# Experts' weights in 2 MB pieces with 16 KB runs: nine whole buffers, and rows and columns taken in fours

## The chip, the core and the metric

The kernel runs on one core of a Trainium2 chip. The metric is the device time of one execution in microseconds (us). TensorE (PE) does the matmuls; before each of them it loads a stationary operand, which the profile lists apart as PEld. VectorE is DVE, ScalarE is ACT, GpSimd is POOL. SyncE (SP) issues nearly all transfers from the chip's memory (HBM) into the on-chip memory of 128 partitions (SBUF). MB here is 1,048,576 bytes, and KB 1,024.

## What is computed

One layer of an encoder on 272 rows, 16 meta tokens and 256 inputs; only the 256 are returned, so only they go through the experts here: two mixers side by side (attention and a state-space scan), an output projection, a layer norm, then a mixture of 32 experts of which each row takes four, and a last layer norm. The change touches the experts alone:

```python
def expert_block(args):                       # one block of rows of one expert e
    tok, g, e = args
    xb = t_pad[tok]
    gate = xb @ w_gate[e] + b_gate[e]         # 1024 x 1024, fp32, as are the next two
    up   = xb @ w_up[e] + b_up[e]
    gate = jnp.minimum(gate, 7.0)
    up   = jnp.clip(up, -7.0, 7.0)
    y = ((up + 1.0) * gate * jax.nn.sigmoid(gate * 1.702)) @ w_down[e] + b_down[e]
    return (y * g[:, None]).astype(t.dtype)
```

The weights of 32 experts are 32 x 3 x 4 MB = 384 MB, and every one of them is read once in a run.

## The kernel before

**Two halves.** Until about 190 us the mixers, the projections and the router run. Then the experts follow, in 32 *positions*. A position is one expert, chosen at run time by how many rows it got, with one or more *units* of 128, 64 or 32 row slots (6, 13 and 14 units in all). For each position the work on PE is: gather the rows, gate, up, and down of the position before.

**The stream of weights.** SP loads the weights in the order gate and up of position t, then down of position t - 1. A piece is 1 MB: 256 rows of a 1024 x 1024 matrix, two whole rows in each of the 128 partitions, so one run of 8 KB per partition. The `ring` of lines 515 to 516 names 19 half buffers of 1 MB; the tiles in them are called wx. They stand on the places of tiles of the first half of the kernel, so the ring comes free one by one. `chunk` (lines 530 to 557) issues one piece, `load_to` (line 559) issues up to a count. A piece may be issued when the piece 19 places before it has been read for the last time, that is, when PE has finished two of the eight blocks of 128 rows (`kb`) of that matrix. The very last piece is issued as two of 512 KB. Four slots (0, 2, 5, 8: `HALVED`) are two tiles of 1 MB each, the others one tile of 2 MB; half of slot 9 is the 19th piece, its other half holds tables.

**The three matmuls.** `linear` (line 1188): the rows are stationary, the weights move. One fp32 matmul stands in the trace as two records, each with a load of its own. With 128 slots, the outputs are two runs of 512 columns. With 64 slots two groups of PE columns work on 512 weight columns each, and with 32 slots four groups on 256 columns each (*quarters*), so the result of a 32-slot unit is folded into 128 partitions x 256 columns.

**Whose row is where.** Since a partition holds neighbouring rows 2p and 2p + 1 of a piece, block kb of the contraction holds rows 256 j + 2p + k. Whatever multiplies the weights must be laid out alike. `rows_of` (line 511) gives these rows as a slice with a step of two columns, 8 bytes apart, and it is used in two places as stationary operand: `token_cols` (line 1151), which gathers the rows of a group of units and turns them (matmuls of `hr` with a one-hot matrix, line 1157: 8 blocks x 2 halves x 2 records = 32 loads in a group, 16 groups), and `transposed` (line 1229), which turns the result of gate and up before down (line 1236: one load per block of 128, 2 for a unit of 32, 4 for one of 64, 8 for one of 128).

**Order.** Each engine's order is that of the code. SP's queue is one: a piece that waits for its buffer holds all pieces behind it. Behind position 28 a loop (`overflow`, line 1305) does what exceeds the slots; SP enters it too, so a limit on `load_to` keeps the pieces issued ahead of it to those that PE still needs there and a few more. `linear` on PE waits for each piece's transfer.

Of the kernel before, what the change touches and what calls it, by code (L numbers as in the profile page):

```python
# [21 lines left out]
D = 1024  # L22
# [42 lines left out]
def hybrid_layer(ctx, tc, I, out):  # L65
# [18 lines left out]
    def slot(i, shape, name, dt=F32):  # L84
        return per.tile(shape, dt, name=name, tag=f"slot{i}")

    HALVED = (0, 2, 5, 8)

    def parts4(i, name, dt=F32):

# [26 lines left out]


    hr = per.tile([128, 2, D], F32, name="hr", tag="hr")
    xs5 = [slot(f"5{c}", [128, 2048], "xs5") for c in "ab"]  # L120
    xm = xs5[1][:16, 1024:2048]
    VR = pt([48, 128], "VR")
    VP = et([48, 128], "VP")
# [48 lines left out]
    s8a, s8b = slot("8a", [128, 2048], "s8a"), slot("8b", [128, 2048], "s8b")  # L172
    oh = s8b[:32, 1600:1600 + NB]
    load(oh, "bucket_onehot", 0, [[NB, 32], [1, NB]])
    load_win("k", 2, 512, 2)
# [294 lines left out]
    BAT = [slot(f"5{c}", [128, 16, 128], "BAT") for c in "ab"]  # L470
    for ri in range(2):
        for a in range(4):
            b = nb()
# [7 lines left out]
                S.activation(BAT[ri][:, 4 * a:4 * a + 4], srcv, AF.Copy)  # L481


    sl0 = slot("0a", [128, 2, D], "sl0")
# [24 lines left out]


    def rows_of(kb):
        a = 256 * (kb // 2) + kb % 2
        return slice(a, a + 255, 2)

    ring = [(9, 0), (6, 0), (6, 1), (3, 0), (3, 1), (4, 0), (4, 1), (2, 0), (8, 0), (2, 1), (8, 1), (1, 0), (1, 1),
            (5, 0), (0, 0), (5, 1), (0, 1), (7, 0), (7, 1)]
    NR = len(ring)
    RT, CH, eid, npools = {}, {}, {}, {}
    stream = []
    for t in range(NE):  # L520
        stream += [(t, w, j) for w in range(2) for j in range(4)]
        if t:
            stream += [(t - 1, 2, j) for j in range(4)]
    stream += [(NE - 1, 2, j) for j in range(4)]
    place = {x_: c for c, x_ in enumerate(stream)}

    def chunk(c):
        t, w, j = stream[c]
        i, half = ring[c % NR]
        if i not in RT:  # L530
            if i == 7:
                t_ = npools["b"].tile([128, 4, D], F32, name="wx", tag="slot7")
                RT[i] = [t_[:, 0:2], t_[:, 2:4]]
            elif i == 9:
                RT[i] = [slot("9a", [128, 2, D], "wx")]
            elif i in HALVED:
                RT[i] = [slot(f"{i}{c}", [128, 2, D], "wx") for c in "ab"]
            else:
                t_ = slot(i, [128, 4, D], "wx")
                RT[i] = [t_[:, 0:2], t_[:, 2:4]]  # L540
        CH[c] = RT[i][half]
        src = I[("w_gate", "w_up", "w_down")[w]]
        if t < 2:
            srcv = pap(src, t * D * D + j * 256 * D, [[2 * D, 128], [1, 2 * D]])
        else:
            if t not in eid:
                eid[t] = SP.value_load(EI[0:1, t:t + 1], min_val=0, max_val=NE - 1)
            srcv = src[0][ds(eid[t], 1), j * 256:(j + 1) * 256, :].rearrange("o (p k) f -> p (o k f)", p=128)
        dstv = CH[c].rearrange("p k f -> p (k f)")
        if c < len(stream) - 1:  # L550
            SP.dma_start(dstv, srcv)
        else:
            for k in range(2):
                SP.dma_start(dstv[:, k * D:(k + 1) * D], srcv[:, k * D:(k + 1) * D])

    nload = [0]

# [2 lines left out]
            chunk(nload[0])  # L560
            nload[0] += 1

    load_to(1)


    def split_w(j, s_, l_, ks):
# [107 lines left out]
    value_rows(0, vt0)  # L674
    states_a(3)
    W_HI, W_LO, W_OUT = {}, {}, {}
    wo1 = [slot(f"2{c}", [128, 2, D], "wo1") for c in "ab"]
    W_OUT[1] = [t_[:, k] for t_ in wo1 for k in range(2)]
    for j in range(2):
        load(wo1[j], "w_out", (512 + 256 * j) * D, [[D, 128], [128 * D, 2], [1, D]])  # L680
    scores_b(2, 0)
    scores_b(2, 1)
    states_b(3)
# [527 lines left out]
    gk = {64: 1, 32: 0}  # L1211

# [16 lines left out]
    def transposed(u_, m):  # L1229
        nf = 128 // m  # L1230
        for a in range(u_.shape[1]):
            nk = u_.shape[2] // 128
            b = 6 + misc[0]
            misc[0] ^= 1
            for k in range(nk):
                T.transpose(PS[:, b, k * 128:k * 128 + 128], u_[:, a, rows_of(k)], ident)  # L1236
            V.tensor_copy(yT[:, 4 * a:4 * a + nk], PS[:, b, :nk * 128].rearrange("p (k s) -> p k s", k=nk))  # L1237
        if m == 128:
            return lambda kb: yT[:, kb]
        q = 8 // nf  # L1240
        return lambda kb: yT[:, kb % q, (kb // q) * m:(kb // q) * m + m]
# [63 lines left out]
    def overflow():  # L1305
        n = nc.values_load(nover[0:1, 0:1], min_val=0, max_val=64)
        with tc.For_i(0, n) as i:  # L1307
            m = 64
            e = SP.value_load(tabi[0:1, 1, ds(i, 1)], min_val=0, max_val=NE - 1)
            t = V.value_load(tabi[0:1, 0, ds(i, 1)], min_val=0, max_val=NE - 1)  # L1310
            pc, gc = wt([128, 2], "pc"), wt([128, 2], "gc")
            th = wt([128, 1], "th")
            V.tensor_copy(th, tabs[:, 1, ds(i, 1)])
            V.tensor_copy(pc, PMs[:, :, ds(t, 1)].rearrange("p a b -> p (a b)"))
            V.tensor_copy(gc, Gs[:, :, ds(t, 1)].rearrange("p a b -> p (a b)"))
            V.tensor_scalar(pc, pc, th, None, op0=OP.subtract)
            sel = wt([96, 128], "si", BF, bufs=3)
            V.tensor_copy(sel[:, :m], P96[:, ds(t, 1)].to_broadcast([96, m]))
            oh_, go = wt([128, 2, 128], "ohp", bufs=2), wt([128, 2, 128], "gop")
            for a in range(2):  # L1320
                V.tensor_scalar(oh_[:, a, :m], io[:, :m], pc[:, a:a + 1], None, op0=OP.is_equal)
                V.tensor_scalar(go[:, a, :m], io[:, :m], pc[:, a:a + 1], gc[:, a:a + 1], op0=OP.is_equal, op1=OP.mult)
            xg = wt([128, 8, 128], "xgp", tag="xg1")
            token_cols(xg, oh_, m)
            gt = gate_rows(go, m)

            def streamed(w):
                tiles = {}
# [32 lines left out]
    def out_pos(t):  # L1361
        for u in pos_units[t]:
            unit_out(u)
        for g in range(NG):
            if last_pos[g] == t:
                combine(g)
        if t == LOOP_AT:
            sum_pending()
            overflow()
        load_to(place[t, 2, 3] + 1 + NR)  # L1370

    def first_done():
        sort_b()
# [178 lines left out]
```

## Time and profile before

| | before |
|---|---|
| median of 3 runs | 1146.16 us (1142.4 to 1146.54) |
| profiled execution: own time | 1143.38 us |
| profiled execution: span of the trace | 1141.6 us |
| mean granted PE clock | 0.95 |
| PE busy | 1022.5 us, 90 % |
| PE weight loads (PEld) | 527.3 us, 46 % |
| weight pieces (gate, up, down) | 128 + 128 + 127 of 1 MB, 2 of 512 KB |
| one piece from issue to landing | 19.7 to 19.8 us |
| moved from HBM | 423.5 MB (of 10^6 bytes), 373 GB/s over the span |

The span runs from the first to the last instruction; the execution's own time is 1.8 us longer. Views of the trace used below: *busy by stretch* (for a stretch of the span, its length, then for each engine the busy us and in brackets the instructions, the granted clock of PE, where 1.00 is 2.4 GHz and 0.50 is 1.2 GHz, the busy share of the DMA engines, GB/s); *waits* (who waited, for whom, us in total, times, the longest); *groups of instructions by shape* (line, engine, operation, output<-input, partitions x elements, count, then busy us, mean ns of one, then idle time before them and what ended it). A load's mean ns is its latency; loads and matmuls overlap, so what one costs a busy PE is read from how often the next begins.

### The profile page before, as it was taken

To read this page: it belongs to the slowest core of one execution; us is meant where nothing else is said; L and a number is where in the kernel's file an instruction comes from. 1 tells how busy PE (TensorE), PEld (TensorE's weight loads), DVE (VectorE), ACT (ScalarE), POOL (GpSimd) and SP (SyncE) were. 2 spreads that over 40 slices of the span, in tenths; PEclk is the share of its full clock that TensorE was granted. 3 is DMA by queue.
4 is the path that set the end of the run, shared out by engine and by line. 5 is a ranking of instruction groups with operands and counts; after the bars stand their busy time and mean duration, and the time that the engine had idled before them with its cause. 6 is when DMAs were issued, how large, how long until landed. Compare 5 with 4: busy or idle time off the path is not lost. (4 is left out here: it accounts for less than half of the span.)

```text
span 1141.6 us, 16410 instructions
## 1 busy us (share of the span) xinstructions
PE 1022.5 (90%) x6572; PEld 527.3 (46%) x6572; DVE 365.6 (32%) x755; ACT 159.6 (14%) x329; POOL 106.5 (9%) x223
## 2 busy tenths in 40 slices
PE   6986997899999788997999977799999999998665
PEld 5865884344554344445444433344453444453222
DVE  7999664222122212321131221122222212222103
ACT  1734423000010000111001000010000000001000
POOL 2300004101100110021001010101101010010001
PEclk9999897999999989998999988999999999999779
DMA  7824286999999999999999999999999999999894
GB/s 220 288 96 167 94 341 253 385 375 420 421 421 421 421 420 420 422 420 421 421 421 420 420 421 420 421 421 421 421 421 421 421 421 394 423 419 420 329 419 195
DMA packets 72313, 425.67 MB, mean 373 GB/s; under 512 B 14925, under 2 KB 15546, under 8 KB 23210
## 3 DMA queue, kind: packets, MB, share of 16 engines
q1 hardware_dynamic: 72234, 424.58, 91.3%
q8 instruction: 53, 0.87, 0.3%
q14 instruction: 26, 0.21, 0.1%
HBM read 423.50 MB, written 1.87 MB: 373 GB/s over the span
## 5 line engine op out<-in xcount | busy, mean ns | idle before, releaser
L1204 PE MATMUL PS<-wx,xgp 128*32 128x256 f32 (+2 forms) x3008 | 484.3, 492 | 38.8 <-DMA wx<-in_w_gate 19.5
L1204 PEld LDWEIGHTS PS<-wx,xgp 128*32 128x32 f32 (+2 forms) x3008 | 185.0, 133 | 296.4 <-issue 203.0
L1204 PE MATMUL PS<-wx,yT 128*32 128x256 f32 (+2 forms) x1504 | 231.0, 473 | 8.8 <-DMA wx<-in_w_down 8.0
L1204 PEld LDWEIGHTS PS<-wx,yT 128*32 128x32 f32 (+2 forms) x1504 | 91.5, 129 | 133.6 <-issue 93.4
L946 POOL COPY si<-P 96x32 bf16<-96x32 bf16 (+2 forms) x32 | 7.4, 233 | 754.8 <-PE PS L1198 724.9
L1251 DVE COPY yc<-PS 32x256 f32<-32x256 f32 (+1 forms) x39 | 20.0, 514 | 159.6 <-ACT yc L1253 159.6
L1157 PEld LDWEIGHTS PS<-ohp,hr 128*128 128x128 f32 x512 | 65.8, 206 | 9.6 <-issue 9.6
L1157 PE MATMUL PS<-ohp,hr 128*128 128x128 f32 x512 | 68.1, 294 | 0.2 <-DVE ohp L1149 0.2
L1226 DVE TENSOR_SCALAR PS<-PS 128x256 f32<-128x256 f32 (+2 forms) x33 | 22.6, 684 | 123.4 <-PE PS L1204 123.4
L1198 PE MATMUL PS<-B,si 96*32 96x256 bf16 (+2 forms) x282 | 40.4, 340 | 16.7 <-SPq L1307 9.7
L1220 DVE TENSOR_SCALAR g<-PS 128x256 f32<-128x256 f32 (+1 forms) x27 | 14.9, 553 | 114.4 <-PE PS L1204 100.6
L1253 ACT ACTIVATE yc<-PS 32x256 f32<-32x256 f32 (+1 forms) x39 | 17.4, 446 | 239.0 <-PE PS L1204 232.7
L1237 DVE COPY yT<-PS 128x512 f32<-128x512 f32 (+1 forms) x39 | 22.7, 594 | 85.6 <-PE PS L1236 85.6
L1288 DVE SCALAR_TENSOR_TENSOR lo<-yc,gc,hi 128x1024 fp32r<-128x1024 f32 x15 | 19.3, 1285 | 86.7 <-ACT hi L1287 85.5
L1302 DVE TENSOR_TENSOR acc<-PS,acc 128x1024 f32<-128x1024 f32 x30 | 35.4, 1220 | 16.6 <-PE PS L1299 16.4
L1161 ACT ACTIVATE xgp<-PS 128x512 f32<-128x512 f32 x16 | 9.6, 598 | 216.4 <-PE PS L1157 216.4
L1198 PEld LDWEIGHTS <-si 96*32 96x32 bf16 (+2 forms) x282 | 11.5, 102 | 50.3 <-issue 47.8
L1147 POOL TENSOR_SCALAR gop<-io,PMs,Gs 128x32 f32<-128x32 f32 (+2 forms) x60 | 33.1, 565 | 0.0
L1221 ACT ACTIVATE PS<-g 128x256 f32<-128x256 f32 (+1 forms) x27 | 13.2, 491 | 138.4 <-DVE g L1220 138.4
L1220 DVE TENSOR_SCALAR yc<-PS 128x1024 f32<-128x1024 f32 x6 | 7.3, 1225 | 78.4 <-PE PS L1204 78.4
L1299 PE MATMUL PS<-hi,gt 128*128 128x512 f32 x60 | 26.6, 443 | 3.0 <-ACTq L1307 3.0
L1299 PE MATMUL PS<-lo,gt 128*128 128x512 f32 x60 | 25.1, 419 | 0.7 <-DVE lo L1288 0.7
(389 smaller groups left out, 845.9 us busy)
## 6 DMA issues: line engine op xcount, KB each, us to landing
wx<-in_w_gate SPq DMA_DIRECT2D x128, 1024.0 KB, 19.8
wx<-in_w_up SPq DMA_DIRECT2D x128, 1024.0 KB, 19.8
wx<-in_w_down SPq DMA_DIRECT2D x127, 1024.0 KB, 19.7
w_u<-in_w_in SPq DMA_DIRECT2D x2, 1024.0 KB
w_q<-in_w_in SPq DMA_DIRECT2D x1, 2048.0 KB
w_k<-in_w_in SPq DMA_DIRECT2D x2, 1024.0 KB
w_v<-in_w_in SPq DMA_DIRECT2D x1, 2048.0 KB
wo<-in_w_out SPq DMA_DIRECT2D x2, 1024.0 KB
```

The source lines that it names most:

```text
L1147: eng.tensor_scalar(dst[:, i, o:o + m], iv, pc, gg[:, i, t:t + 1], op0=OP.is_equal, op1=OP.mult)
L1157: T.matmul(PS[:, 4 + h, k * 128:k * 128 + n], hr[:, i, rows_of(db)], oh_[:, i, :n], start=(i == 0), stop=(i == 1))
L1198: T.matmul(o, sel[:, :m], B96[:, w, f * n:f * n + n], start=True, stop=False)
L1204: T.matmul(PS[(f % nf) * m:(f % nf) * m + m, b + f // nf, :n], xT(kb), c[:, f * n:f * n + n], start=False, stop=(kb == 7))
L1220: V.tensor_scalar(g_, r_, 7.0, None, op0=OP.min)
L1226: V.tensor_scalar(r_, r_, 7.0, -7.0, op0=OP.min, op1=OP.max)
L1237: V.tensor_copy(yT[:, 4 * a:4 * a + nk], PS[:, b, :nk * 128].rearrange("p (k s) -> p k s", k=nk))
L1251: V.tensor_copy(d_, s_)
L1253: S.activation(d_, s_, AF.Copy)
L1288: V.scalar_tensor_tensor(lo[:n], YC[g][:n], GC[g][:n], hi[:n].bitcast(F32), op0=OP.mult, op1=OP.subtract)
L1299: T.matmul(PS[:, 4 + 2 * i + h], GT[g][:n, i * 128:(i + 1) * 128], part[:n, h * 512:(h + 1) * 512], start=(j == 0), stop=(j == 1))
L1302: V.tensor_tensor(acc[:, i].rearrange("p (h c) -> p h c", h=2), PS[:, 4 + 2 * i:6 + 2 * i], acc[:, i].rearrange("p (h c) -> p h c", h=2), ...
```

## The change

Pieces become 2 MB: 512 rows, four neighbouring rows per partition, one run of 16 KB in HBM and in SBUF. The ring is nine whole buffers of 2 MB (18 MB in all); half of slot 9 is no longer used, and no slot is halved (`HALVED = ()`). A matrix is then two pieces, and a buffer comes free when PE has finished four blocks. The first piece is issued behind two transfers of `w_out` instead of ahead of them. The last piece is issued as 1 MB, 512 KB, 512 KB.

Block kb now holds rows 512 j + 4p + k. So `rows_of` steps by four columns, 16 bytes; the load in `token_cols` does, and that in `transposed` for units of 64 and 128 slots. For units of 32 slots the load in `transposed` keeps a step of two, because the quarters of gate and up are taken otherwise: quarter f holds two of every four columns of its half (`cols`, `place_of`), so the moving operand reads pairs of columns, 8 bytes of every 16. Down keeps whole quarters. The loop behind position 28 reads its rows to match.

```diff
-    HALVED = (0, 2, 5, 8)
+    HALVED = ()
...
     def rows_of(kb):
-        a = 256 * (kb // 2) + kb % 2
-        return slice(a, a + 255, 2)
-
-    ring = [(9, 0), (6, 0), (6, 1), (3, 0), (3, 1), (4, 0), (4, 1), (2, 0), (8, 0), (2, 1), (8, 1), (1, 0), (1, 1),
-            (5, 0), (0, 0), (5, 1), (0, 1), (7, 0), (7, 1)]
+        a = 512 * (kb // 4) + kb % 4
+        return slice(a, a + 509, 4)
+
+    ring = [6, 3, 4, 2, 8, 1, 5, 0, 7]
...
     for t in range(NE):
-        stream += [(t, w, j) for w in range(2) for j in range(4)]
-        if t:
-            stream += [(t - 1, 2, j) for j in range(4)]
-    stream += [(NE - 1, 2, j) for j in range(4)]
+        stream += [(t, w, j) for w in range(2) for j in range(2)]
+        if 0 < t < NE:
+            stream += [(t - 1, 2, j) for j in range(2)]
+    stream += [(NE - 1, 2, j) for j in range(2)]
...
-            srcv = src[0][ds(eid[t], 1), j * 256:(j + 1) * 256, :].rearrange("o (p k) f -> p (o k f)", p=128)
+            srcv = src[0][ds(eid[t], 1), j * 512:(j + 1) * 512, :].rearrange("o (p k) f -> p (o k f)", p=128)
...
-        if c < len(stream) - 1:
-            SP.dma_start(dstv, srcv)
-        else:
-            for k in range(2):
-                SP.dma_start(dstv[:, k * D:(k + 1) * D], srcv[:, k * D:(k + 1) * D])
+        for k0, k1 in (((0, 4),) if c < len(stream) - 1 else ((0, 2), (2, 3), (3, 4))):
+            SP.dma_start(dstv[:, k0 * D:k1 * D], srcv[:, k0 * D:k1 * D])
...
-    load_to(1)
...
-    load_to(19)
+    load_to(9)
...
+        def cols(a, f):
+
+            if m > 32 or w == 2:
+                return a[:, f * n:f * n + n]
+            return a[:, f // 2 * 512:f // 2 * 512 + 512].rearrange("p (q e k) -> p e q k", e=2, k=2)[:, f % 2]
+
+        def place_of(f):
+            o = PS[(f % nf) * m:(f % nf) * m + m, b + f // nf, :n]
+            return o if m > 32 or w == 2 else o.rearrange("p (q k) -> p q k", k=2)
...
             for f in range(1024 // n):
-                T.matmul(PS[(f % nf) * m:(f % nf) * m + m, b + f // nf, :n], xT(kb),
-                         c[:, f * n:f * n + n], start=False, stop=(kb == 7))
+                T.matmul(place_of(f), xT(kb), cols(c, f), start=False, stop=(kb == 7))
...
     def in_place(t, w):
-        return lambda kb: CH[place[t, w, kb // 2]][:, kb % 2]
+        return lambda kb: CH[place[t, w, kb // 4]][:, kb % 4]
...
-                T.transpose(PS[:, b, k * 128:k * 128 + 128], u_[:, a, rows_of(k)], ident)
+                T.transpose(PS[:, b, k * 128:k * 128 + 128], u_[:, a, slice(k, k + 127 * nk + 1, nk)], ident)
...
-            n = place[t, w, 3] + 1 + NR
-            load_to(min(n, place[LOOP_AT, 2, 3] + 1 + 4) if t == LOOP_AT + 1 else n)
+            n = place[t, w, 1] + 1 + NR
+            load_to(min(n, place[LOOP_AT, 2, 1] + 1 + 2) if t == LOOP_AT + 1 else n)
```

PE's order is the same before and after: 1192 rows of the same operations on the same shapes, of which only the buffers' and lines' numbers differ. SP's order shrinks from 897 rows to 537. On SP, where the first pieces go between the other loads of the first half (MG, wo, wr, cr, bf are tables and matrices of the mixers and the router), before:

```order
L128 DMA MG<-in_w_glu 128x4x512
L551 DMA wx<-in_w_gate 128x2048
L128 DMA wo_794<-in_w_out 128x2x1024
L128 DMA wo_795<-in_w_out 128x2x1024
L551 DMA wx<-in_w_gate 128x2048 x2
L128 DMA wo_983<-in_w_out 128x4x1024
L128 DMA wr<-in_w_router 128x8x32
```

and after:

```order
L129 DMA MG<-in_w_glu 128x4x512
L129 DMA wo_787<-in_w_out 128x2x1024 x2
L547 DMA wx<-in_w_gate 128x4096
L129 DMA wo_974<-in_w_out 128x4x1024
L129 DMA wr<-in_w_router 128x8x32
```

Of three pieces of 1 MB, one ahead of wo and two behind it, there is now one piece of 2 MB behind it.

On SP again, where it enters the loop behind position 28 (nover is the count that the loop reads; the view names the ISA rows no further), before:

```order
L551 DMA wx<-in_w_gate 128x2048
L551 ISA
L551 DMA wx<-in_w_up 128x2048
L551 ISA
L551 DMA wx<-in_w_up 128x2048
L551 ISA
L551 DMA wx<-in_w_up 128x2048
L1306 TENSOR_LOAD nover
L1306 ISA x2
```

and after:

```order
L547 DMA wx<-in_w_gate 128x4096
L547 ISA
L547 DMA wx<-in_w_up 128x4096
L1307 TENSOR_LOAD nover
L1307 ISA x2
```

Before, three of the four MB of up of position 30 are issued ahead of the loop, and 21 MB remain behind it (1 + 5 matrices of 4 MB); now two of the four are, and 22 MB remain.

## Rows read from the trace of the kernel before

**Rows 1.** Busy by stretch, the experts' half (columns as told in the section above).

```profile
186.00:246.00 60.00, 55.25 (x281) 25.64 (x282) 17.79 (x57) 5.22 (x10) 8.27 (x15) 0.92 0.83 313
246.00:380.00 134.00, 132.89 (x964) 63.05 (x962) 35.65 (x50) 12.69 (x22) 9.12 (x22) 1.00 1.01 421
380.00:738.00 358.00, 314.19 (x2291) 147.75 (x2288) 73.62 (x110) 29.33 (x56) 30.68 (x72) 0.95 1.01 421
738.00:1040.00 302.00, 300.40 (x1539) 138.41 (x1540) 72.36 (x92) 27.47 (x46) 21.75 (x50) 0.99 1.01 418
1067.00:1120.00 53.00, 40.16 (x390) 15.18 (x382) 6.40 (x14) 3.77 (x9) 0.32 (x2) 0.82 0.99 406
```

**Rows 2.** SP's waits, 190 to 268 us: who waited for whom, total us, times, longest.

```profile
SPq L551 <- PE PS L1204: 73.5, 32, 20.3
```

**Rows 3.** SP's waits, 268 to 718 us.

```profile
SPq L551 <- DMA wx<-in_w_gate: 116.4, 60, 3.0
...
SPq L551 <- PE PS L1204: 7.4, 20, 1.6
```

**Rows 4.** Instructions in time, 713 to 724 us: start, us, what, idle before it.

```profile
720.67 3.67 PE L1204 MATMUL PS<-wx,xgp 128*128 128x512 f32 x8 [0.95 <-DMA wx<-in_w_gate]
```

**Rows 5.** SP's waits, 738 to 1040 us.

```profile
SPq L551 <- PE PS L1204: 62.6, 47, 5.5
```

**Rows 6.** Busy by stretch, 32 to 40 us: runs of 2 KB.

```profile
32.00:40.00 8.00, 6.30 (x31) 5.25 (x30) 7.45 (x32) 7.79 (x24) 7.01 (x22) 1.00 1.05 395
```

**Rows 7.** Transfers of 28 to 42 us: packets by size.

```profile
DMA packets 2293, 4.27 MB, mean 305 GB/s; under 512 B 193, under 2 KB 254, under 8 KB 2292
```

**Rows 8.** Weight loads by shape, whole span: busy us, mean ns, idle before.

```profile
L1157 PEld LDWEIGHTS PS<-ohp,hr 128*128 128x128 f32 x512 | 65.8, 206 | 9.6 <-issue 9.6
...
L1204 PEld LDWEIGHTS PS<-wx,yT 128*128 128x128 f32 x192 | 36.5, 190 | 43.9 <-issue 43.1
...
L1236 PEld LDWEIGHTS PS<-ident,g 128*128 128x128 f32 x80 | 12.1, 206 | 18.3 <-issue 9.8 <-DVE acc L1302 7.7 <-DVE g L1222 0.8
...
L475 PEld LDWEIGHTS PS<-ident,AB 128*128 128x128 f32 x32 | 3.6, 141 | 0.1
```

**Rows 9.** Line 1157, one group: ns least/median/most, first and last start.

```profile
L1157 PE MATMUL PS<-ohp,hr x32: 272/281/282, 754.1 to 757.8; 128*128 128x128 f32 x32
```

**Rows 10.** Line 837 on DVE, which writes 16 bytes apart.

```profile
L837 DVE SCALAR_TENSOR_TENSOR gy<-y,y x4: 626/634/636, 139.2 to 144.8; 128x256 f32<-128x256 f32 x4
```

**Rows 11.** Line 1227 on DVE, neighbouring elements, by shape.

```profile
L1227 DVE SCALAR_TENSOR_TENSOR g<-PS,g 128x512 f32<-128x512 f32 x13 | 9.0, 691 | 0.4
...
L1227 DVE SCALAR_TENSOR_TENSOR g<-PS,g 128x256 f32<-128x256 f32 x14 | 5.9, 424 | 0.5
```

**Rows 12.** Groups by shape, 185 to 246 us.

```profile
L1157 PEld LDWEIGHTS PS<-ohp,hr 128*128 128x128 f32 x64 | 9.3, 229 | 1.9 <-issue 1.9
...
L1236 PEld LDWEIGHTS PS<-ident,g 128*128 128x128 f32 x4 | 0.6, 208 | 0.8 <-issue 0.8
```

**Rows 13.** Groups by shape, 246 to 718 us.

```profile
L1204 PE MATMUL PS<-wx,xgp 128*32 128x256 f32 x1280 | 88.9, 417 | 27.8 <-DMA wx<-in_w_gate 13.9 <-DMA wx<-in_w_up 13.8
...
L1157 PEld LDWEIGHTS PS<-ohp,hr 128*128 128x128 f32 x256 | 33.2, 209 | 4.2 <-issue 4.2
...
L1236 PEld LDWEIGHTS PS<-ident,g 128*128 128x128 f32 x42 | 6.4, 206 | 10.6 <-issue 5.1 <-DVE acc L1302 5.1 <-DVE g L1222 0.4
...
L1236 PEld LDWEIGHTS PS<-ident,yc 128*128 128x128 f32 x24 | 3.1, 209 | 2.6 <-DVE acc L1302 2.6
```

**Rows 14.** Groups by shape, 738 to 1049 us.

```profile
L1157 PEld LDWEIGHTS PS<-ohp,hr 128*128 128x128 f32 x192 | 23.3, 196 | 3.5 <-issue 3.5
...
L1204 PE MATMUL PS<-wx,xgp 128*32 128x256 f32 x256 | 15.0, 380 | 0.0
...
L1236 PEld LDWEIGHTS PS<-ident,g 128*128 128x128 f32 x26 | 3.9, 204 | 5.3 <-DVE acc L1302 2.6 <-issue 2.2 <-DVE g L1222 0.4
...
L1236 PEld LDWEIGHTS PS<-ident,yc 128*128 128x128 f32 x24 | 3.1, 209 | 2.4 <-DVE acc L1302 2.4
```

More of the change, by code (lines that the diff above doesn't have):

```diff
@@ L119, in hybrid_layer @@
     hr = per.tile([128, 2, D], F32, name="hr", tag="hr")
-    xs5 = [slot(f"5{c}", [128, 2048], "xs5") for c in "ab"]
+    xs5w = slot(5, [128, 4096], "xs5")
+    xs5 = [xs5w[:, 2048 * j:2048 * j + 2048] for j in range(2)]
     xm = xs5[1][:16, 1024:2048]
@@ L171, in hybrid_layer @@
     load(rb, "rel_bias", 0, [[4, 32], [1, 4]])
-    s8a, s8b = slot("8a", [128, 2048], "s8a"), slot("8b", [128, 2048], "s8b")
+    s8 = slot(8, [128, 4096], "s8")
+    s8a, s8b = s8[:, :2048], s8[:, 2048:]
     oh = s8b[:32, 1600:1600 + NB]
@@ L469, in hybrid_layer @@
     S.activation(kT[:, 0, :], proj("k", 0, 0), AF.Copy)
-    BAT = [slot(f"5{c}", [128, 16, 128], "BAT") for c in "ab"]
+    BATw = slot(5, [128, 2, 16, 128], "BAT")
+    BAT = [BATw[:, j] for j in range(2)]
     for ri in range(2):
@@ L481, in hybrid_layer @@
                 S.activation(BAT[ri][:, 4 * a:4 * a + 4], srcv, AF.Copy)
-    sl0 = slot("0a", [128, 2, D], "sl0")
+    sl0 = slot(0, [128, 2, D], "sl0")
     bc = slot("9b", [128, 2, D], "bc")
@@ L528, in chunk @@
         t, w, j = stream[c]
-        i, half = ring[c % NR]
+        i = ring[c % NR]
         if i not in RT:
             if i == 7:
[L532 to L537, printed above, removed]
-            else:
-                t_ = slot(i, [128, 4, D], "wx")
-                RT[i] = [t_[:, 0:2], t_[:, 2:4]]
-        CH[c] = RT[i][half]
+                RT[i] = npools["b"].tile([128, 4, D], F32, name="wx", tag="slot7")
+            else:
+                RT[i] = slot(i, [128, 4, D], "wx")
+        CH[c] = RT[i]
         src = I[("w_gate", "w_up", "w_down")[w]]
         if t < 2:
-            srcv = pap(src, t * D * D + j * 256 * D, [[2 * D, 128], [1, 2 * D]])
+            srcv = pap(src, t * D * D + j * 512 * D, [[4 * D, 128], [1, 4 * D]])
         else:
@@ L676, in hybrid_layer @@
     W_HI, W_LO, W_OUT = {}, {}, {}
-    wo1 = [slot(f"2{c}", [128, 2, D], "wo1") for c in "ab"]
-    W_OUT[1] = [t_[:, k] for t_ in wo1 for k in range(2)]
+    wo1 = slot(2, [128, 4, D], "wo1")
+    W_OUT[1] = [wo1[:, k] for k in range(4)]
     for j in range(2):
-        load(wo1[j], "w_out", (512 + 256 * j) * D, [[D, 128], [128 * D, 2], [1, D]])
+        load(wo1[:, 2 * j:2 * j + 2], "w_out", (512 + 256 * j) * D, [[D, 128], [128 * D, 2], [1, D]])
     scores_b(2, 0)
@@ L731, in hybrid_layer @@
     lag_b()
-    load_to(3)
+    load_to(1)
     vt1 = values(3)
@@ L747, in hybrid_layer @@
     value_rows(3, vt1)
-    load_to(5)
+    load_to(2)
     cat = mt([128, 8, NT], "cat", FR, tag="hTcat")
@@ L850, in hybrid_layer @@
     out_a(3)
-    load_to(7)
+    load_to(3)
     out_c(0)
@@ L926, in hybrid_layer @@
     bc1 = [wt([128, D], "bc1", tag=f"xg{j}") for j in range(2)]
-    load_to(11)
+    load_to(5)
     load(bc1[0], "ln1_g", 0, [[0, 128], [1, D]])
     load(bc1[1], "ln1_b", 0, [[0, 128], [1, D]])
-    load_to(13)
+    load_to(6)
     G.iota(jp, pattern=[[1, 128]], base=0, channel_multiplier=-1)
@@ L1032, in hybrid_layer @@
     mix(1, (7,), (1,))
-    load_to(17)
+    load_to(8)
     mid.close()
@@ L1195, in linear @@
         b = linb(nbk)
+        def cols(a, f):
[5 more added lines that the diff above has]
+            return o if m > 32 or w == 2 else o.rearrange("p (q k) -> p q k", k=2)
         for f in range(1024 // n):
-            o = PS[(f % nf) * m:(f % nf) * m + m, b + f // nf, :n]
-            T.matmul(o, sel[:, :m], B96[:, w, f * n:f * n + n], start=True, stop=False)
+            T.matmul(place_of(f), sel[:, :m], cols(B96[:, w], f), start=True, stop=False)
         for kb in range(8):
@@ L1332, in get @@
                     src = I[("w_gate", "w_up", "w_down")[w]]
-                    j = kb // 2
-                    two = src[0][ds(e, 1), j * 256:(j + 1) * 256, :].rearrange("o (p k) f -> p (o k f)", p=128)
-                    SP.dma_start(tiles[kb], two[:, kb % 2 * D:(kb % 2 + 1) * D])
+                    j = kb // 4
+                    four = src[0][ds(e, 1), j * 512:(j + 1) * 512, :].rearrange("o (p k) f -> p (o k f)", p=128)
+                    SP.dma_start(tiles[kb], four[:, kb % 4 * D:(kb % 4 + 1) * D])
                     return tiles[kb]
@@ L1369, in out_pos @@
             overflow()
-        load_to(place[t, 2, 3] + 1 + NR)
+        load_to(place[t, 2, 1] + 1 + NR)
     def first_done():
```

## Prediction

> **What bounds the kernel now.** I read busy time by stretch first, then the waits of SP's queue, then the groups by shape in each stretch. The experts' half falls into four parts. From 186 to 246 us PE works 55.25 of 60 us while the transfers move only 313 GB/s [rows 1]; SP waits 73.5 us for the matmuls of line 1204 in this part and its neighbourhood, once 20.3 us [rows 2]: all buffers are full and PE frees them, so PE is the bound. From 246 to 738 us the queue moves 421 GB/s without a break, and PE stands idle 1.1 + 43.8 = 44.9 us [rows 1]; SP waits on transfers, hardly ever on PE (7.4 us) [rows 3]: the transfers are the bound, with PE close behind. At 720.67 us position 19 begins with a wait of 0.95 us for its first piece [rows 4]; it is the last for 300 us. From 738 to 1040 us PE works 300.40 of 302 us [rows 1], and SP again waits for line 1204, 62.6 us in 47 waits [rows 5]: PE is the bound, though the transfers run at 418 GB/s. Behind the loop, from 1067 us, PE is idle a quarter of the time and the transfers move 406 GB/s [rows 1]: what remains of the stream sets the end. So anything that makes PE's own work longer counts whole in the first and third part, and a faster stream counts in the second and the last.
>
> **Longer runs.** With runs of 2 KB (2038 of 2293 packets of that stretch are between 2 and 8 KB) the queue moves 395 GB/s [rows 6, 7], with runs of 8 KB 421 [rows 1]. Per run on one of 16 engines that is 83.0 and 311.3 ns, on a line 6.9 ns + 38.05 ns per KB; 16 KB would take 615.7 ns, or 2.463 us per MB against 2.491. From 246 to 721 us some 190 MB move: 190 x 0.028 = **-5.3 us**. Bounds: 0, and -10.6 if the fixed 6.9 ns vanished altogether.
>
> **Fewer, larger buffers.** 18 MB instead of 19 are ahead of PE while it is the bound, so the stream enters the second part one MB (2.5 us) later; and a buffer comes free after four blocks, not two, by which the first MB of a pair waits for the second. I take **+3.3** (2.5 to 5). Where PE waits for a transfer, it waits for the whole 2 MB before it can start on the first block: at position 19 [rows 4] the second MB comes 2.5 us after the first, **+2.5** (0 to 2.5). In the second part this wait repeats at each new piece, but PE's idle time there is already the stream's and isn't added. The first piece's later place in SP's queue is hidden: the stream comes to stand before full buffers anyway [rows 2]. SP's 360 fewer rows save nothing, since SP waits.
>
> **The step of four as stationary operand.** This is the large term. The load of line 1157 takes 206 ns with its step of 8 bytes, the plain load of the same size 190 ns; of the transposes, the load with a step of 8 bytes takes 206 ns and that of neighbouring columns 141 ns [rows 8]. So a transposed load pays 65 ns for reaching over 1024 bytes instead of 512, 2.0 ns for every further 16 bytes. On DVE, line 837 writes its 256 elements 16 bytes apart in 634 ns [rows 10]; neighbouring ones take 424 ns, and 691 ns for 512, so 157 ns + 1.04 ns each [rows 11]; those 16 bytes apart take (634 - 157)/256 = 1.86 ns each. A price per 16 bytes reached, about 1.9 ns, fits both engines. In a group of 32 loads of line 1157 one begins every 3.7/31 = 0.119 us [rows 9], which is 64 x 1.86 ns: the load of 1024 bytes can be what sets this pace. With a step of 16 bytes it reaches over 2048 bytes, and the pace would be 0.238 us: +0.119 for each load whose step doubles (0.141 by the transposes' 2.0 ns; 0 if the price is for having a step at all, the first rival). I take 0.119, since it fits line 1157 itself.
>
> The Trainium skill, SBUF — State Buffer, section Specifications (TRN2), gives this memory lines of 16 bytes and asks for two hits on a line for full bandwidth. By that rule a step of four columns loses and a step of two doesn't; the trace agrees only in part, since the step of two already costs 65 ns in the transposes. By the rule alone the pairs below, with two hits on each line, would cost nothing, and the sum would be +40.3 instead of +40.8.
>
> Now the counts. First part: 64 loads of line 1157 and 4 transposes, all of 64 slots [rows 12], 68 x 0.119 = 8.1; some stand behind the last release that the queue waits for, so **+6.8** (6.2 to 8.1). Second part: 256 loads and 42 + 24 transposes, of which 18 belong to nine units of 32 slots and keep their step [rows 13]: 304 x 0.119 = 36.2 us of PE work, against 44.9 us of idle time. The cover is there, but not evenly: from 246 to 380 us PE is idle for only 1.1 us [rows 1], and as long as the ring is still full at its start, what PE loses there the queue loses. I take **+3** (0 to 8). Third part: 192 loads and 26 + 24 transposes, 6 of them of 32 slots [rows 14]: 236 x 0.119 = **+28.1** (33.3 at 0.141), with nothing to hide it.
>
> **Pairs as moving operand.** A quarter reads 256 columns in pairs, so over 128 x 16 bytes: 128 x 1.86 = 238 ns a pass at most, against 3.67 us for eight records of 512 columns, some 0.43 us each or 0.22 for 256 [rows 4]: up to 8 % on gate and up of 32 slots. Four such linears of 64 records stand in the third part, 15.0 us [rows 14]; I take 3 %, **+0.5** (0 to 1.2). The 20 in the second part (88.9 us [rows 13]) add 2.7 us to PE's work there, within the same cover.
>
> **The end.** SP issues one MB less ahead of the loop, so 22 MB instead of 21 follow it: +2.5 - 21 x 0.028 = **+1.9**. The last pieces are as fine as before (512 KB). PE in the loop and behind it waits for transfers and hides its own loads.
>
> **Sum.** -5.3 + 3.3 + 2.5 + 6.8 + 3 + 28.1 + 0.5 + 1.9 = +40.8 us. The profiled execution took 1143.4 us, 2.8 below the median of three; the mean of all four is 1144.6. 1144.6 + 40.8 = **1185 us**. With the terms' bounds, which won't all fall to one side, 1172 to 1198.
>
> **The rivals.**
> *A step costs once.* The 65 ns of the transposes might be the price of any step, 8 bytes or 16, and DVE's writes say nothing of PE's reads. For it: a plain fp32 load takes 190 ns and the one with a step 206, so line 1157 hardly shows a price per byte. Against it: 1.86 and 2.0 ns agree. Then 6.8, 3 and 28.1 fall away, and -5.3 + 3.3 + 2.5 + 0.5 + 1.9 = +2.9: **1147.5 us** (1140 to 1153), not slower by anything that can be told. It holds from the point where a group of line 1157 keeps its 3.7 us.
> *The stream's gain comes through.* The same, with the fixed 6.9 ns gone and the 18 MB and pairs hidden: -10.6 + 2.4 = **1136 us**. Against it: SP's 62.6 us of waits in the third part [rows 5] show that a faster stream would only wait longer.
> *Pairs are slow too.* The four groups of columns read at once, 4 x 256 columns in the time of one. If neighbouring quarters hinder each other in the same 16 bytes and a pass takes twice as long, the third part gets 15.0 us more and the second 88.9 more against cover that the loads have nearly used up: 1185 + 15 + 80 = **1280 us**, or 1230 at half of it. Against it: a group takes only 8 of 16 bytes in 1.86 ns now.
>
> **How the numbers follow.** My forecast 0.67, a step costs once 0.20 (0.16 within 0.5 %, 0.01 faster, 0.03 slower), the stream's gain 0.05, slow pairs 0.08. Half a per cent, 5.7 us, is about what a measurement of this kernel can tell from no change. Faster 0.01 + 0.05 = 0.06; same 0.16; slower 0.67 + 0.03 + 0.08 = 0.78. The range must reach to the first rival, since the forecast alone holds less than 8 in 10: 1142 to 1200, which leaves out the slow pairs, the gain, and the edges.
>
> **What the profile would show.** Loads of line 1157 some 110 to 130 ns longer than 206, and a group of 32 taking 7.4 us instead of 3.7; the transposes of 64 and 128 slots alike, and those of 32 slots at 206. The stretch from position 19 to the loop longer by 28 us with PE still never idle; PE's idle time in the second part down to some 10 us; 424 to 426 GB/s in the second part. The forecast falls if the loads stay near 206 ns, if a group keeps its 3.7 us (the load then hides behind its matmul), or if the moving passes of 32 slots exceed 0.24 us.

## The result, and the profile after

| | before | after |
|---|---|---|
| median of 4 runs | 1145.02 us (1142.4 to 1146.54) | 1171.65 us (1170.59 to 1173.02) |
| profiled execution: own time, span | 1143.38, 1141.6 us | 1173.02, 1171.2 us |
| PE busy | 1022.5 us | 1078.0 us |
| PE weight loads | 527.3 us | 592.6 us |
| mean granted PE clock | 0.950 | 0.957 |

The changed kernel takes 1.0234 times the time of the kernel before (95 % interval 1.0212 to 1.0256): 26.6 us more by the medians, 29.6 by the two spans. Busy time by stretch in the changed kernel, in the columns of [rows 1] (length, then PE, PEld, DVE, ACT, POOL, the granted clock, the DMA engines' share, GB/s):

```profile
186.00:246.00 60.00, 54.27 (x245) 29.68 (x246) 17.94 (x61) 4.83 (x10) 8.44 (x16) 0.90 0.77 302
246.00:380.00 134.00, 133.46 (x838) 66.11 (x835) 30.67 (x43) 10.72 (x20) 8.90 (x21) 1.00 0.98 413
380.00:738.00 358.00, 336.96 (x2442) 175.59 (x2441) 77.32 (x115) 30.87 (x58) 30.88 (x72) 0.98 1.00 424
738.00:1040.00 302.00, 298.05 (x1268) 145.77 (x1270) 69.08 (x82) 25.15 (x40) 21.54 (x49) 0.99 0.94 388
1067.00:1120.00 53.00, 39.14 (x331) 16.80 (x330) 10.87 (x16) 5.14 (x10) 1.10 (x2) 0.83 0.92 385
```

Against [rows 1]: PE's idle time from 246 to 738 us has fallen from 44.9 us to 0.5 + 21.0. From 738 us on the transfers move only 388 GB/s, 0.94 of their time, where they were at 1.01 and 418 before: they wait for PE. SP's waits from 738 to 1040 us, where it waited 62.6 us for these matmuls before [rows 5]:

```profile
SPq L547 <- PE PS L1206: 252.6, 51, 11.1
```

The weight loads by shape, as in [rows 8], where the gather's line 1157 is now 1149, the transposes' 1236 now 1237, and 1204 now 1206:

```profile
L1149 PEld LDWEIGHTS PS<-ohp,hr 128*128 128x128 f32 x512 | 121.1, 329 | 8.5 <-issue 7.9
...
L1206 PEld LDWEIGHTS PS<-wx,yT 128*128 128x128 f32 x192 | 36.5, 190 | 43.9 <-issue 43.0
...
L1237 PEld LDWEIGHTS PS<-ident,g 128*128 128x128 f32 x80 | 12.1, 206 | 19.0 <-issue 10.6 <-DVE acc L1303 7.5 <-DVE g L1223 0.9
...
L478 PEld LDWEIGHTS PS<-ident,AB 128*128 128x128 f32 x32 | 3.6, 141 | 0.1
```

The gather's load takes 329 ns instead of 206, and its busy time has gone from 65.8 to 121.1 us. The transposes, whose step was doubled too for units of 64 and 128 slots, stay at 206 ns. The beginning of position 19 (start, us, instruction), and one group of the gather as in [rows 9] (ns least/median/most, first and last start):

```profile
728.17 4.10 PE L1206 MATMUL PS<-wx,xgp 128*128 128x512 f32 x9
...
L1149 PE MATMUL PS<-ohp,hr x32: 273/397/398, 761.7 to 768.8; 128*128 128x128 f32 x32
```

Position 19 begins at 728.17 us instead of 720.67 [rows 4], and no longer waits for a transfer. The 32 starts of a group span 7.1 us, one every 0.229 us; before, they spanned 3.7 us, one every 0.119 [rows 9]. Of the six groups in the third part (the eleventh to the sixteenth of the run) each pushes the rest back by some 3.7 us: they begin 7.6, 11.2, 14.9, 18.4, 22.1 and 26.5 us later than before, and the loop is entered 30.2 us later.

### The profile page after: what moved, and what is told of

Read it like the earlier page. It is cut to its first block, busy times and chain, and to the rows that moved or that the text cites. A ratio compares the mean times of both kernels' runs of the same rounds, so it can differ in the third digit from the quotient of the medians.

```text
span 1171.2 us, 15679 instructions
## 1 busy us (share of the span) xinstructions
PE 1078.0 (92%) x6572; PEld 592.6 (51%) x6572; DVE 366.0 (31%) x755; ACT 159.5 (14%) x329; POOL 106.5 (9%) x223
## 5 line engine op out<-in xcount | busy, mean ns | idle before, releaser
L1206 PEld LDWEIGHTS PS<-wx,xgp 128*32 128x32 f32 (+2 forms) x3008 | 189.2, 131 | 275.4 <-issue 207.6
L1149 PEld LDWEIGHTS PS<-ohp,hr 128*128 128x128 f32 x512 | 121.1, 329 | 8.5 <-issue 7.9
L1149 PE MATMUL PS<-ohp,hr 128*128 128x128 f32 x512 | 122.7, 399 | 0.2 <-DVE ohp L1141 0.2
L1238 DVE COPY yT<-PS 128x512 f32<-128x512 f32 (+1 forms) x39 | 22.7, 594 | 85.7 <-PE PS L1237 85.7
L1221 DVE TENSOR_SCALAR g<-PS 128x256 f32<-128x256 f32 (+1 forms) x27 | 14.9, 553 | 96.6 <-PE PS L1206 96.5
```

What stands on the lines that cost most here:

```text
L1149: T.matmul(PS[:, 4 + h, k * 128:k * 128 + n], hr[:, i, rows_of(db)], oh_[:, i, :n], start=(i == 0), stop=(i == 1))
L1206: T.matmul(place_of(f), xT(kb), cols(c, f), start=False, stop=(kb == 7))
L1221: V.tensor_scalar(g_, r_, 7.0, None, op0=OP.min)
```

## The experiments

All edits are against the kernel named. Times stand beside runs of the kernel before on the same chip.

### The steps by themselves

The layer is left out; each stretch is 32 matmuls (64 records) or 32 transposes of one shape, with four plain matmuls ahead of it. This is the core of it in short, with s for the steps 1, 2, 4, 8 that the run spells out:

```diff
+    def st(i, k, s):
+        return hr[:, i, slice(k % s, k % s + 127 * s + 1, s)]
+    for r in range(32):                       # lines 107, 110, 113, 116
+        T.matmul(PS[:, 2, :128], st(r % 2, r // 2, s), oh[:, r % 2], start=True, stop=True)
+    for r in range(32):                       # lines 119 to 128: 32 moving columns
+        T.matmul(PS[:, 3, :32], st(r % 2, r // 2, s), oh[:, r % 2, :32], start=True, stop=True)
+    for r in range(32):                       # lines 131, 134, 137, 140
+        T.transpose(PS[:, 4, :128], st(r % 2, r // 2, s), ident)
+    for r in range(32):                       # lines 143, 146, 149, 152: 32 rows
+        T.transpose(PS[:, 5, :32], hr[:32, r % 2, slice(r % s, r % s + 127 * s + 1, s)], ident[:32, :32])
+    # moving: runs of 256, pairs of every four, every fourth column
+    #   lines 167, 171, 175: four groups of 32 columns; 179, 183, 187: one group
```

> Leaves the whole layer out: only stretches of 32 equal matmuls (64 records) or 32 transposes, each with another step of the stationary operand (1, 2, 4, 8 columns of 4 bytes), then 32 matmuls whose moving operand is a run of 256 columns, pairs of every four, or every fourth column. Theory A, half rate: a load goes at full rate while two of its elements lie in the same 16 bytes, and at half of it with one; an fp32 load then takes 0.107 us or 0.213, a transposed one 0.05 or 0.107, and it shows only where it exceeds its matmul. So one record begins every 0.12, 0.12, 0.23, 0.23 us with 128 moving columns, every 0.11, 0.11, 0.22, 0.22 with 32; transposes of 128 moving columns every 0.12 at all four steps, those of 32 every 0.055, 0.055, 0.11, 0.11. The forecast's theory, a price for each 16 bytes reached: 0.12, 0.12, 0.24, 0.48 and the transposes of 128 columns the same. Moving operand: four groups of 32 columns, one record each 0.06 us for runs and for pairs under A, 0.12 for every fourth column; slow pairs would be 0.12 too. One group: 0.22, 0.22, 0.43.

Instructions by line (count: least, median, most ns, then the first and the last start in us):

```profile
L107 PEld LDWEIGHTS PS<-oh,hr x64: 190/192/192, 33.2 to 40.6; 128*128 128x128 f32 x64
...
L110 PEld LDWEIGHTS PS<-oh,hr x64: 195/196/197, 43.8 to 51.5; 128*128 128x128 f32 x64
...
L113 PEld LDWEIGHTS PS<-oh,hr x64: 307/329/329, 54.7 to 69.6; 128*128 128x128 f32 x64
...
L116 PEld LDWEIGHTS PS<-oh,hr x64: 312/335/336, 73.0 to 88.2; 128*128 128x128 f32 x64
...
L125 PEld LDWEIGHTS PS<-oh,hr x64: 308/329/329, 121.3 to 136.2; 128*128 128x128 f32 x64
...
L128 PEld LDWEIGHTS PS<-oh,hr x64: 312/335/338, 141.8 to 157.0; 128*128 128x128 f32 x64
...
L131 PEld LDWEIGHTS PS<-ident,hr x32: 139/140/142, 162.4 to 166.1; 128*128 128x128 f32 x32
...
L134 PEld LDWEIGHTS PS<-ident,hr x32: 195/209/209, 169.4 to 173.4; 128*128 128x128 f32 x32
...
L137 PEld LDWEIGHTS PS<-ident,hr x32: 196/212/212, 176.6 to 180.7; 128*128 128x128 f32 x32
...
L140 PEld LDWEIGHTS PS<-ident,hr x32: 188/193/194, 183.9 to 187.7; 128*128 128x128 f32 x32
...
L143 PEld LDWEIGHTS PS<-ident,hr x32: 133/137/138, 191.5 to 193.4; 32*128 32x128 f32 x32
...
L146 PEld LDWEIGHTS PS<-ident,hr x32: 190/211/213, 197.2 to 200.9; 32*128 32x128 f32 x32
...
L149 PEld LDWEIGHTS PS<-ident,hr x32: 191/212/213, 206.5 to 210.2; 32*128 32x128 f32 x32
...
L152 PEld LDWEIGHTS PS<-ident,hr x32: 181/198/202, 216.9 to 220.3; 32*128 32x128 f32 x32
...
L167 PE MATMUL PS<-wx,oh x64: 379/379/404, 227.0 to 230.3; 128*32 128x256 f32 x64
...
L171 PE MATMUL PS<-wx,oh x64: 385/387/413, 234.2 to 237.7; 128*32 128x256 f32 x64
...
L175 PE MATMUL PS<-wx,oh x64: 617/632/633, 241.6 to 248.4; 128*32 128x256 f32 x64
...
L179 PE MATMUL PS<-wx,oh x64: 379/379/379, 252.5 to 266.1; 128*128 128x256 f32 x64
...
L183 PE MATMUL PS<-wx,oh x64: 388/388/390, 269.8 to 284.1; 128*128 128x256 f32 x64
...
L187 PE MATMUL PS<-wx,oh x64: 610/629/630, 287.7 to 316.1; 128*128 128x256 f32 x64
```

The pace is the distance of the first and the last start over the count less one. A full fp32 load: (40.6 - 33.2)/63 = 0.117 us at a step of one, 0.122 at two, 0.237 at four, 0.241 at eight (lines 107 to 116), and the same 0.237 and 0.241 when only 32 columns move behind it (lines 125, 128), so there the load sets the pace (the granted clock was 1.00 in lines 107 to 116 and 0.70 in 125 and 128, and the pace is the same). From four to eight nothing more is paid, though twice the bytes are reached over: the forecast's price for each 16 bytes is refuted. What counts, as far as these rows go, is whether a second element lies in the same 16 bytes (a step of three was not run). Transposes with 128 moving columns begin every 0.119 to 0.132 us at all steps (lines 131 to 140). With 32 rows and columns it is 0.061 us for neighbouring columns, and 0.119, 0.119 and 0.110 at two, four and eight, where the load sets the pace (lines 143, 146, 149, 152). So a transposed load is slow from a step of two on, while theory A (half rate where only one element lies in the 16 bytes) had it slow from four on; why, no run shows. That slowness just fits behind 128 moving columns. Moving operands: a set of four groups begins every 0.22 us in runs, 0.23 in pairs, 0.45 for every fourth column (lines 167, 171, 175: 16 sets of four records, so the distance is taken over 15); one group every 0.216, 0.227, 0.451. Pairs cost some 5 %.

### The gather's step alone, put into the kernel before

```diff
-                    T.matmul(PS[:, 4 + h, k * 128:k * 128 + n], hr[:, i, rows_of(db)],
+                    T.matmul(PS[:, 4 + h, k * 128:k * 128 + n], hr[:, i, slice(512 * (db // 4) + db % 4, 512 * (db // 4) + db % 4 + 509, 4)],
```

> The kernel before with one edit: the gather's load steps by four columns, so the rows reach the weights in another order than theirs. If the step is the cause: +20.7 in the third part and some 6 to 10 ahead of it, 1172 to 1176. If the pieces and buffers are the cause: 1145.

1170.29 us, 1.0217 times before (1.0181 to 1.0253), a little under what was expected of the step. The weight load by shape:

```profile
L1157 PEld LDWEIGHTS PS<-ohp,hr 128*128 128x128 f32 x512 | 121.1, 329 | 9.0 <-issue 8.4
```

It has the busy time and the 329 ns of the changed kernel. The eleventh group begins 8.3 us late and the loop is entered 30.1 us late, against 7.6 and 30.2 with the whole change. With pieces of 1 MB, runs of 8 KB and 19 buffers all of the loss is there.

### The gather's step taken out of the changed kernel

```diff
-                    T.matmul(PS[:, 4 + h, k * 128:k * 128 + n], hr[:, i, rows_of(db)],
+                    T.matmul(PS[:, 4 + h, k * 128:k * 128 + n], hr[:, i, db * 128:(db + 1) * 128],
```

> The changed kernel, but the gather's load reads neighbouring columns, so the rows reach the weights in another order than theirs. If the gather's step is the cause (0.108 us for each of its 512 loads), 20.7 us of the stretch from position 19 to the loop go, and some 6 us ahead of it: 1145 us, 1141 to 1149. If the cause is the 2 MB pieces and fewer buffers, it stays above 1165. If transposes count too, it stays some 5 to 8 us above before, 1151.

1145.49 us, 0.9991 of before (0.9965 to 1.0016). The load:

```profile
L1149 PEld LDWEIGHTS PS<-ohp,hr 128*128 128x128 f32 x512 | 60.8, 197 | 9.3 <-issue 9.3
```

The whole loss is gone. The eleventh group begins 0.3 us, the loop 0.8 us later than in the kernel before; 7.0 us were lost at the fourth group and won back by the tenth.

### The transposes' step alone

```diff
-                T.transpose(PS[:, b, k * 128:k * 128 + 128], u_[:, a, rows_of(k)], ident)
+                T.transpose(PS[:, b, k * 128:k * 128 + 128], u_[:, a, slice(k, k + 127 * nk + 1, nk) if nk == 4 else rows_of(k)], ident)
```

> The kernel before with one edit: the transposes of units of 64 and 128 slots step by four columns, so the result of gate and up reaches down's weights in another order. Theory A: the load stays hidden behind its matmul, 1145 (1143 to 1147). The forecast's price of 0.119 for each: 44 of them in the third part, 5.2 us, and 1 to 3 ahead of it: 1151 to 1153.

1144.47 us, 0.9998 of before (0.9980 to 1.0016). The loads:

```profile
L1236 PEld LDWEIGHTS PS<-ident,g 128*128 128x128 f32 x80 | 12.1, 207 | 18.6 <-issue 10.1 <-DVE acc L1302 7.7 <-DVE g L1222 0.8
...
L1236 PEld LDWEIGHTS PS<-ident,yc 128*128 128x128 f32 x48 | 6.2, 210 | 5.1 <-DVE acc L1302 5.1
```

One nanosecond more at most than in [rows 8] and [rows 13] (206 and 209), and nothing in the end. The forecast's price for the transposes falls.

### Quarters of neighbouring columns in the changed kernel

```diff
-            if m > 32 or w == 2:
+            if True:
                 return a[:, f * n:f * n + n]
...
-            return o if m > 32 or w == 2 else o.rearrange("p (q k) -> p q k", k=2)
+            return o if True else o.rearrange("p (q k) -> p q k", k=2)
```

> The changed kernel with quarters of neighbouring columns again, as before, so the results of 32-slot units reach down's weights in another order. If pairs as moving operand cost nothing: 1171.5 (1169 to 1174). If they cost 3 % of their passes: 1170, which can't be told from nothing. If they are a cause of their own: below 1166.

1174.31 us, 1.0248 times before (1.0224 to 1.0272); the changed kernel's 1.0234 lies within that. Without pairs the time is no shorter, so they are no cause of the loss that this measurement can tell.

### Large buffers with runs of 8 KB

```diff
-                srcv = src[0][ds(eid[t], 1), j * 512:(j + 1) * 512, :].rearrange("o (p k) f -> p (o k f)", p=128)
+                srcv = src[0][ds(eid[t], 1), j * 512:(j + 1) * 512, :].rearrange("o (a p k) f -> p (o a) (k f)", a=2, p=128)
...
-        a = 512 * (kb // 4) + kb % 4
-        return slice(a, a + 509, 4)
+        a = 256 * (kb // 2) + kb % 2
+        return slice(a, a + 255, 2)
```

The quarters, the transposes and the loop's rows go back with it.

> The changed kernel with the rows, steps and quarters of the kernel before: pieces of 2 MB in nine buffers, but each of two runs of 8 KB per partition. It shows the buffers alone. By the forecast's terms: +3.3 for fewer buffers, +2.5 for position 19's wait for a whole piece, +2.5 for the end: 1153 (1146 to 1156). If buffers are the cause of the loss: 1165 or more. If they cost nothing: 1145.

1150.87 us, 1.0069 times before (1.0042 to 1.0097). So the buffers alone cost some 6 us by the medians, 5 to 11 by the interval. Against it, the changed kernel without the gather's step (1145.49) has runs of 16 KB, and that is 5.4 us less by the medians (it also has the stepped transposes and the pairs, which cost nothing that shows). Busy time by stretch, 380 to 738 us, first of this kernel, then of the changed kernel without the gather's step (GB/s is the last column):

```profile
380.00:738.00 358.00, 312.71 (x2342) 150.68 (x2342) 74.32 (x112) 28.30 (x55) 31.05 (x72) 0.95 1.01 421
```

```profile
380.00:738.00 358.00, 314.33 (x2357) 150.95 (x2354) 77.51 (x115) 29.41 (x57) 31.05 (x72) 0.97 1.01 427
```

421 against 427 GB/s.

### A ring of 18 in the kernel before

```diff
-    ring = [(9, 0), (6, 0), (6, 1), (3, 0), ...
+    ring = [(6, 0), (6, 1), (3, 0), ...
...
-    load_to(19)
+    load_to(18)
```

The other counts of `load_to` in the first half fall by one as well.

> The kernel before without the 19th half buffer: 18 pieces of 1 MB, freed and waited for one by one as before. It tells what of the loss of the 2 MB pieces is the smaller ring. If the ring's size is the cause: position 5 begins some 5 us later than in the kernel before, as with the 2 MB pieces, and position 19 3 us later; 1148 to 1151. If the cause is that a buffer comes free only with four blocks and that a whole piece of 2 MB must land: 2.5 us late at most, 1145 to 1147.

1147.30 us, 1.0023 times before (1.0004 to 1.0043). The eleventh group begins 4.0 us late, 3.3 with the pieces of 2 MB. Counted from the first group, which begins 1.4 us late here and 0.8 us early there, that is 4.0 - 1.4 = 2.6 against 3.3 + 0.8 = 4.1: the lost MB is most of what the large buffers cost up to there, and whether the rest comes of their coming free by fours isn't shown. The fourth group is 2.3 us late here and 4.9 there. The rest of the large buffers' 6 us comes at the loop and behind it (5.6 us late at its entry, 7.5 at the end); I didn't separate that further.

### Three pieces less ahead of the loop

```diff
-        load_to(place[t, 2, 3] + 1 + NR)
+        load_to(place[t, 2, 3] + 1 + NR - (3 if t == LOOP_AT - 1 else 0))
```

> The kernel before with three pieces less issued ahead of the loop behind position 28, so that none of up of position 30 goes ahead. In the kernel before PE waits 9.7 us in the loop, since SP enters its work there only when all pieces that it has issued have landed. If so, PE's wait falls by three pieces' 7.5 us to 2 or 3 us, and the three pieces then have to be moved behind the loop: 1144 to 1147 in all, no gain, which is why the changed kernel, too, gives back less than nothing there. If the wait were of another cause: it stays 9.7 us, and the time rises by 7 us to 1152.

1143.60 us, 0.9998 of before (0.9981 to 1.0015). What PE waited for from 1049 us on (us in total, times, longest):

```profile
PE PS L1204 <- DMA wx<-in_w_up: 9.0, 5, 3.9
PE PS L1204 <- DMA wx<-in_w_down: 5.4, 6, 1.5
PE PS L1204 <- DMA wx<-in_w_gate: 3.9, 4, 1.4
...
PE PS L1198 <- DVEq L1307: 2.4, 1, 2.4
```

The same view of the kernel before:

```profile
PE PS L1198 <- SPq L1307: 9.7, 1, 9.7
PE PS L1204 <- DMA wx<-in_w_up: 4.6, 3, 3.9
PE PS L1204 <- DMA wx<-in_w_gate: 3.7, 4, 1.4
...
PE PS L1204 <- DMA wx<-in_w_down: 3.0, 5, 1.2
```

The wait for SP in the loop (9.7 us) is gone, one of 2.4 us is left in its place, and the waits for pieces behind it have grown from 11.3 to 18.3 us. In the trace of the kernel before, SP comes to the loop at 1046.3 us and waits there until 1065.4, when the last piece that it had issued lands; PE goes on at 1066.4. The wait in the loop was one for transfers that had been issued; it can be moved, not saved.

### The changed kernel with the rows written in the gather's order

```diff
-        eng.tensor_tensor(hf, hf, bc1[1][:, h * 512:(h + 1) * 512], op=OP.add)
+        eng.tensor_tensor(hp[:, i, h * 512:(h + 1) * 512].rearrange("p (k q) -> p q k", k=4),
+                          hf.rearrange("p (q k) -> p q k", k=4),
+                          bc1[1][:, h * 512:(h + 1) * 512].rearrange("p (q k) -> p q k", k=4), op=OP.add)
...
-                    T.matmul(PS[:, 4 + h, k * 128:k * 128 + n], hr[:, i, rows_of(db)],
+                    T.matmul(PS[:, 4 + h, k * 128:k * 128 + n], hp[:, i, db * 128:(db + 1) * 128],
```

hp is a tile in the half of slot 9 that the ring no longer uses; the residual sum reads it back with the step undone.

> The changed kernel, same results, but the rows are written once in the order in which the gather reads them, into the 1 MB that the ring no longer uses (line 970 writes with a step, four instructions), so the gather's load reads neighbouring columns. If the gather's step is the cause and the runs of 16 KB keep their gain: 1143 (1138 to 1148), the same as before or up to 0.6 % faster. If the stepped writes delay the first gather: 1 to 2 us of it lost again. If the pieces are the cause: above 1165.

1145.37 us, 1.0004 times before (0.9983 to 1.0025): the change without its loss, and no faster than before. The stepped writes cost nothing that shows. I ran no version that beats the kernel before.

## Why the prediction held, and where its terms were off

The sum by place, in the two profiles, against the kernel before:

| up to | forecast | measured |
|---|---|---|
| position 19's first matmul | -5.3 + 3.3 + 2.5 + 6.8 + 3 = +10.3 | +7.5 |
| entry of the loop | +28.1 + 0.5 = +28.6 | +22.7 |
| end | +1.9 | -0.6 |
| whole span | +40.8 | +29.6 |

Two profiles differ by a microsecond or two at the same place for no reason of the change: the gather's first group begins 1.1 us later in the changed kernel than before, and in the other runs between 0.8 us earlier and 1.8 us later.

**The bound.** Right. From position 19 to the loop PE was the bound, and what its loads gained in length came out whole: 192 loads, and their group's busy time went from 23.9 to 45.7 us, +21.8; the four linears with pairs went from 15.0 to 15.8 us, +0.8 (3 % was taken, some 5 % is what the steps by themselves show, too). That is the 22.7.

**The step of four, the large term.** Right in place and sign, mis-sized by 6 us, and for a wrong reason. The price per load was 21.8/192 = 0.114 us where 0.119 was taken, 1.0 us of the difference. The other 5.2 us are the 44 transposes, which cost nothing. The step that failed is the one that read 65 ns between two *latencies* in [rows 8] as the reading of 512 more bytes, and made of it a price for every 16 bytes. By that price a step of eight would have cost 0.48 us in line 116, and it costs 0.241. DVE's 1.86 ns, which seemed to confirm it, wasn't tested again. The loads of transposes at a step of two already go at half rate, and don't get slower at four. They hid behind their matmuls before, and their pace would have shown it: 0.119 to 0.132 us at every step, neighbouring columns too. The gather's load went at full rate at a step of two, and at half at four. Its 0.119 us before was its matmul's pace as much as its own. The sum came near because the load at half rate, 0.237 us, is about the double of that pace: that was luck, since the wrong rule and the right one meet at a step of four. The term's upper bound was also worked out wrongly: 64 x 2.0 ns is 0.13 us a load, not 0.141, and 33.3 would have been 30.7.

The Trainium skill, SBUF — State Buffer, section Specifications (TRN2), asks for two hits in 16 bytes for full bandwidth. The fp32 loads and the moving operands agree: 0.122 us at two hits and 0.237 at one, 0.227 and 0.451. The loads of transposes don't: 0.061 us with four hits, 0.119 with two as with one.

**Ahead of position 19.** The third group begins 8.7 us late, 1.7 without the step. Counted from the first group the first part lost 7.7 us, 7.4 with the step alone and 0.5 without it: the step's 7 us and a little more stand against the 6.8 forecast. The runs of 16 KB were sized a little low: 427 GB/s, where 615.7 ns a run would be 425.7, so 190 MB win some 7 us, not 5.3. The fewer buffers cost 3.3 to 4.0 us by the eleventh group (2.6 to 4.1 counted from the first) for the 3.3 taken. The +2.5 for the wait of a whole piece at position 19 didn't come: with PE later, the piece is there. The cover in the second part held: of 44.9 us of idle time, 21.6 are left, and the lag, 12.4 us at the fourth group and 14.7 at the ninth, was 7.2 at the tenth. But the forecast saw some 10 us left. Between the starts of the third group and the eleventh the gather's busy time grew by 27.0 us (34.3 to 61.3), less than the 36.2 forecast, mostly since the transposes cost nothing, and the rest of PE's busy time fell by 8.0 us (383.1 to 375.0); what made it fall, no run shows. The +3 for what it would not hide was not needed at the end.

**The end.** Forecast +1.9, measured -0.6. What was overlooked is the loop: before, PE waits 9.7 us in it, because SP goes to work there only when what it has issued has landed. With PE 30 us later these transfers have landed sooner in comparison: the last lands at 1089.0 us, 6.8 behind PE's entry, where it was 13.4 before (1065.4 and 1052.0). From the loop's entry on, the changed kernel's PE waited:

```profile
PE PS L1206 <- DMA wx<-in_w_down: 6.4, 3, 2.9
PE PS L1206 <- DMA wx<-in_w_up: 6.0, 3, 3.2
PE PS L1206 <- DMA wx<-in_w_gate: 3.6, 2, 2.9
...
PE PS L1200 <- SPq L1308: 2.9, 1, 2.9
```

2.9 us in the loop, 6.8 less, and 16.0 us for pieces, 4.7 more: 2.1 us less in all. The 22nd MB is in these. The 1.5 us between that and the -0.6 weren't followed.

**The rivals.** A step that costs once holds for the transposes, but not for the gather, on which it had to be decided: the starts of its group span 7.1 to 7.3 us. Slow pairs fell: some 5 %, and 0.227 us a pass where 0.24 was the sign. The stream's gain didn't come through: without the gather's step it is 5.4 us, and the smaller ring takes it back.

The profiled execution of the changed kernel was its slowest of four, 1.4 us above the median, that of before 1.6 below; hence 29.6 between the profiles and 26.6 between the medians.

## What to carry to other kernels

A layout that makes transfers better is paid for where the other operand has to follow it. Count the elements that lie in the same 16 bytes for every access that the new layout touches, and look whether the engine has room for half the rate there. Read the price of a load from the pace of a long row of them, never from its latency, and from a row in which the load sets the pace; a few equal instructions run alone show it. And 1.5 % of a stream's rate was worth 5.4 us of 1145 here, by the medians; the smaller ring of larger buffers that it took cost about as much.

## What the runs showed of the hardware that was not expected

The load of a transpose is twice as slow at a step of two columns as at one, and no slower at four or eight, while a plain fp32 load is as fast at two and half as fast at four; eight columns cost either no more than four. Moving operands keep to the same rule as fp32 loads, also with four column groups at once (0.22, 0.23, 0.45 us a set).

Where 32 columns moved behind each fp32 load, the granted clock fell to a mean of 0.77, 0.88, 0.70 and 0.70 in the four stretches, though PE never paused. Neighbouring columns (line 119) and a step of four (line 125), each first while 1.00 (2.4 GHz) was granted, then while 0.50 (1.2 GHz) was:

```profile
L119 PEld LDWEIGHTS PS<-oh,hr x41: 190/192/192, 91.5 to 96.3; 128*128 128x128 f32 x41
...
L119 PEld LDWEIGHTS PS<-oh,hr x21: 333/333/338, 96.7 to 100.9; 128*128 128x128 f32 x21
...
L125 PEld LDWEIGHTS PS<-oh,hr x25: 308/329/329, 121.3 to 127.1; 128*128 128x128 f32 x25
...
L125 PEld LDWEIGHTS PS<-oh,hr x39: 329/329/329, 127.4 to 136.2; 128*128 128x128 f32 x39
```

The paces are 0.120 and 0.210 us for neighbouring columns, 0.242 and 0.232 for a step of four. So it isn't PE's clock that limits a load at a step of four, and while 0.50 is granted that step costs only some 0.02 us a load.
